# A hybrid decoder layer on one core: the input projection in column groups of 272, 512 and 256 instead of 272, 384 and 384, with padded activation rows

## The chip, the core and the metric

The kernel runs on one core of one Trainium2 chip. A core has a matrix engine (PE, TensorE), a vector engine (DVE, VectorE), a scalar engine (ACT, ScalarE), a general engine (POOL, GpSimd) and a queue that issues transfers (SP, SyncE). They share an on-chip memory of 128 partitions (SBUF); PE writes its results to a second one (PSUM), which is used in banks of 512 fp32 values for each partition. The metric is the device time of one execution in microseconds. Before the change it is 1302.69 us, the median of three runs from 1301.43 to 1303.88.

## The reference

One layer: 16 meta tokens are put in front of 1024 tokens, so there are L = 1040 rows. They are normalised and projected to seven groups of columns, which feed two mixers side by side; then come an output projection and a feed-forward network with a short convolution.

```python
h = jnp.concatenate([meta, x], axis=1)
a = rmsnorm(h, ln_mix_pre[l])
proj = a @ w_in[l]
dq, dk, dv, hq, hf, hi, hg = jnp.split(proj, SPLITS, axis=-1)
y_diff = diff_attention(dq, dk, dv, ...)
y_hgrn = hgrn2(hq, hf, hi, hg, ...)          # uses silu(hg) as a gate
mix = jnp.concatenate([y_diff, y_hgrn], axis=-1) @ w_out[l]
h = h + rmsnorm(mix, ln_mix_post[l])
a = rmsnorm(h, ln_ffn_pre[l])
y = conv_ffn(a, w_ffn_up[l], ffn_conv_w[l], ffn_conv_b[l], w_ffn_down[l])
h = h + rmsnorm(y, ln_ffn_post[l])
```

All data are fp32. There are 4 attention heads (dq, dk, dv) and 4 recurrent heads (hq, hf, hi, hg); each of the seven has 128 columns for a head.

## The kernel before

**Tiles.** The 1040 rows are 9 blocks, one of 16 and eight of 128. The normalised rows are kept transposed: `ahi` and `alo` hold, for each of 8 slices k of the 1024 features, 1040 columns; `ahi` is the value rounded to PE's fast fp32 form, `alo` what the rounding left. The weights are split in the same way into a high and a low part (`load_split`: ACT casts the high part, POOL subtracts). A product then takes three matmuls for each k: high by high (L241), high by low (L243), low by high (L245). One projected tile is 128 columns of the result by all 1040 rows, and is made in three column groups (`GROUPS`): blocks 0 to 2 (272 columns), 3 to 5 (384) and 6 to 8 (384). `proj_group` takes a PSUM bank of the tag `ip` for a group, issues its 24 matmuls through `proj_step`, and then calls the tile's own function (`evac`) that copies the result out. There are 28 such tiles, seven for each of the four heads.

**Stages.** Head 0's dq, dk and dv are made while the rows are still being normalised and transposed. This stage's beginning is written out by hand with the class `Kinds` (L893): group 0 of the three tiles and group 1 of dq, between the transposes (L280) of blocks 3, 4 and 5. Then `head0(1)` is interleaved with blocks 6 to 8 (`pre_blocks`), and `head0(2)` with the tables of the position bias. Then, for each head h, the tiles hf, hq, hi and hg are interleaved with the attention of head h, and dq, dk and dv of head h+1 with the recurrence of head h. In these stages there are two banks of the tag `ip`, so a group may start once the group before the last has been copied out. The output projection follows (L1020, L1022, L1024), in two halves of 512 columns (n = 0 and 1), with its weights loaded and split by `load_wo`; then the feed-forward network (L1383 to L1385 up, L1543 to L1545 down).

**Order.** PE's instructions run in the order in which the code issues them; `interleave` hands out dense matmuls against the small ones by a cost in ns. The other engines' order is chosen by a scheduler from a model of costs, except for the written-out beginning. So a change in widths or buffers can move instructions on ACT, DVE and POOL that the diff doesn't name.

**Names that the prediction uses.** xs is a block of rows: ACT squares and sums it (`pre_stat`), takes ln and exp of the sum ss, DVE scales it (`pre_scale`), PE transposes it into px (`pre_turn`), ACT and DVE copy px to `ahi` and `alo`. sg and gate belong to hg: `ev_g` runs exp on ACT, a bound on DVE, two more steps on ACT and the product with the PSUM bank on DVE. woh, wol and wor are the high part, the low part and the raw load of the output weights, wh_dk and wr_dk the same for dk's; ws and ra are sums and raw loads of the up weights. Raw loads of weights go round a ring of three buffers (tag `wr`). The split output weights n = 0, k = 2 to 4 and n = 1, k = 6 and 7 lie in a pool of their own (`wosplit`), opened ahead of `ahi` and `alo`; those of n = 0, k = 0 and 1 lie with the other weights, and the rest in a pool that is opened when `ahi` and `alo` are gone, and so have to wait for the last dense matmul.

## Time and profile before

| what | value |
|---|---|
| median of 3 runs | 1302.69 us |
| lowest, highest | 1301.43, 1303.88 us |
| time of the profiled execution | 1300.73 us |
| its span | 1298.9 us |
| PE busy | 1268.1 us, 98% |
| DVE, ACT, POOL busy | 887.0, 695.1, 482.6 us |

The span runs from the first to the last instruction that the profiler saw. A row of the timeline gives the start in us, the duration in us, the engine, the line, the operation, what is written from what, the shape and the number of like instructions; in brackets stands how long the engine was idle before, and what ended the idle time. L53 is the line of a helper through which all of ACT's, DVE's and POOL's instructions pass, so these are told apart by their tiles. Rows of the table by stage give, after the length, the busy time and the number of instructions of PE, of PE's weight loads, DVE, ACT and POOL, then the granted clock of PE as a share of full speed, the DMA engines' busy share and the GB/s. Rows of the waits give the waiting engine and line, what it waited for, the total in us, the number of waits and the longest. A row of one tile gives the number of instructions, the least, median and greatest duration in ns, the first and last start, and the shapes.

### The profile page before, as it was taken

How to read it: one execution, taken by the hardware profiler on the slowest of the kernel's cores; microseconds unless marked ns; L12 is line 12 of the kernel's file. 1: busy time of each engine (PE TensorE's matmuls, PEld its weight loads, DVE VectorE, ACT ScalarE, POOL GpSimd, SP SyncE). 2: the span in 40 equal slices, each digit the busy share in tenths (PEclk: the TensorE clock that was granted, in tenths of full speed). 3: DMA queues.
4: the chain of work that ended last, by engine and by line, in shares of the span. 5: the costliest groups of instructions: out<-in, count | busy, mean ns of one | idle time of the engine just before them, and what ended most of it. 6: DMA issues, size and time to landing. Idle time of an engine off the chain costs nothing.

```text
span 1298.9 us, 26100 instructions
## 1 busy us (share of the span) xinstructions
PE 1268.1 (98%) x10154; PEld 1179.0 (91%) x10154; DVE 887.0 (68%) x1488; ACT 695.1 (54%) x1639; POOL 482.6 (37%) x387
## 2 busy tenths in 40 slices
PE   8999999999999999999999999999999999999996
PEld 7999999899999998767899999999999998888885
DVE  7574646465645574547897877778778767697686
ACT  8465466546654764356854544544445435554553
POOL 5231423242323310353066575666665731010121
PEclk9999999999999999999999999999999999999999
DMA  6244655182644532787312222222222128964263
GB/s 215 94 99 89 120 120 116 47 156 78 125 116 86 122 103 90 222 272 265 117 67 82 90 75 82 74 89 83 74 75 90 66 79 274 336 203 170 90 211 122
DMA packets 116418, 165.04 MB, mean 127 GB/s; under 512 B 10099, under 2 KB 57523, under 8 KB 116294
## 3 DMA queue, kind: packets, MB, share of 16 engines
q1 hardware_dynamic: 93062, 151.84, 35.1%
q0 software_dynamic: 23232, 11.54, 7.6%
q8 instruction: 80, 1.31, 0.4%
q14 instruction: 44, 0.36, 0.1%
HBM read 134.24 MB, written 52.17 MB: 144 GB/s over the span
## 4 chain that ended last, share of the span: by engine, by line
PE 46%; DVE 4%; ACT 2%; issue 1%; DMA 1%; DVEq 0%; ACTq 0%
PE pd L1544 5%; PE pd L1545 5%; PE pd L1543 5%; PE pb L1383 5%; PE pb L1384 4%; PE pb L1385 4%; PE pa L1384 3%; PE pa L1383 3%; PE pa L1385 3%; PE pc L1384 3%; PE pc L1383 3%; PE pc L1385 3%; DVE c L53 1%; DVE t L53 1%; DVE xh L53 1%
## 5 line engine op out<-in xcount | busy, mean ns | idle before, releaser
L1383 PE MATMUL pb<-t,uh 128*128 128x258 f32 x504 | 142.5, 283 | 2.9 <-DVE u L53 2.7
L1384 PE MATMUL pb<-t,uh 128*128 128x258 f32 x504 | 141.2, 280 | 0.0
L1385 PE MATMUL pb<-t,ul 128*128 128x258 f32 x504 | 141.0, 280 | 0.0
L1544 PE MATMUL pd<-wl,gh 128*128 128x512 f32 x308 | 120.5, 391 | 2.0 <-DVE wl L53 2.0
L1545 PE MATMUL pd<-wh,gl 128*128 128x512 f32 x308 | 120.0, 390 | 0.0
L1543 PE MATMUL pd<-wh,gh 128*128 128x512 f32 x308 | 120.0, 390 | 0.0
L53 DVE SCALAR_TENSOR_TENSOR c<-uu,cwt,c 128x514 f32<-128x514 f32 (+1 forms) x88 | 96.5, 1096 | 19.6 <-ACT c L53 18.9
L53 POOL TENSOR_TENSOR c<-c,c 128x514 f32<-128x514 f32 (+1 forms) x44 | 63.8, 1449 | 122.3 <-ACT c L53 120.2
L1383 PEld LDWEIGHTS pb<-t,uh 128*128 128x128 f32 x504 | 95.0, 189 | 5.3 <-DVE u L53 5.3
L1385 PEld LDWEIGHTS pb<-t,ul 128*128 128x128 f32 x504 | 95.3, 189 | 0.0
L1384 PEld LDWEIGHTS pb<-t,uh 128*128 128x128 f32 x504 | 95.0, 188 | 0.0
L1384 PE MATMUL pa<-t,uh 128*128 128x258 f32 (+1 forms) x336 | 94.7, 282 | 0.0
L1383 PE MATMUL pa<-t,uh 128*128 128x258 f32 (+1 forms) x336 | 94.6, 281 | 0.0
L1385 PE MATMUL pa<-t,ul 128*128 128x258 f32 (+1 forms) x336 | 94.3, 281 | 0.0
L1384 PE MATMUL pc<-t,uh 128*128 128x258 f32 (+1 forms) x336 | 94.1, 280 | 0.0
L1385 PE MATMUL pc<-t,ul 128*128 128x258 f32 (+1 forms) x336 | 94.1, 280 | 0.0
L1383 PE MATMUL pc<-t,uh 128*128 128x258 f32 (+1 forms) x336 | 93.9, 279 | 0.0
L53 DVE SCALAR_TENSOR_TENSOR c<-ug,cwt,c 128x514 f32<-128x514 f32 (+1 forms) x88 | 88.3, 1004 | 1.4 <-ACT c L53 0.6
L53 ACT CAST uh<-ra 128x512 fp32r<-128x512 f32 x67 | 41.1, 617 | 63.2 <-PE pb L1384 42.0
L53 DVE TENSOR_TENSOR ul<-ra,uh 128x512 fp32r<-128x512 f32 x42 | 40.2, 957 | 48.7 <-ACT uh L53 48.7
L53 POOL TENSOR_TENSOR ul<-ws,uh 128x512 fp32r<-128x512 f32 x42 | 60.4, 1437 | 34.4 <-ACT uh L53 33.7
L1544 PEld LDWEIGHTS pd<-wl,gh 128*128 128x128 f32 x308 | 57.8, 188 | 15.5 <-DVE wl L53 3.7
(388 smaller groups left out, 4167.1 us busy)
## 6 DMA issues: line engine op xcount, KB each, us to landing
ra<-in_wup_dram SPq DMA_DIRECT2D x88, 256.0 KB, 2.6
mp<-msc SPq DMA_DIRECT2D x23, 512.0 KB, 5.0
tsc<-in_wdown_dram SPq DMA_DIRECT2D x44, 256.0 KB, 4.5
wi<-tsc SPq DMA_DIRECT2D x44, 256.0 KB, 2.7
gi<-gsc SPq DMA_DIRECT2D x33, 256.0 KB, 4.4
wi<-in_wdown_dram SPq DMA_DIRECT2D x33, 256.0 KB, 5.2
gsc<-c SPq DMA_DIRECT2D x22, 257.0 KB, 2.0
tsc<-in_wdown_dram POOLq DMA_DIRECT2D x22, 256.0 KB, 7.4
```

The lines of the kernel that those rows point to most:

```text
L53: ins = call(*args, **kw)
L1383: T.matmul(pt, hi[:, s], th[:, k], start=(first and k == 0), stop=False, skip_group_check=True)
L1384: T.matmul(pt, hi[:, s], tl[:, k], start=False, stop=False, skip_group_check=True)
L1385: T.matmul(pt, lo[:, s], th[:, k], start=False, stop=(k == 3), skip_group_check=True)
L1543: T.matmul(py, gh[:, s], wh, start=(k == 0 and pr not in (3, 7)), stop=False, skip_group_check=True)
L1544: T.matmul(py, gh[:, s], wl, start=False, stop=False, skip_group_check=True)
L1545: T.matmul(py, gl[:, s], wh, start=False, stop=(k == NH - 1), skip_group_check=True)
```

## The change

The 25 tiles outside head 0's dq, dk and dv are made in groups of 272, 512 and 256 columns (`SPANS`), those three in four groups of 272, 256, 256 and 256 (`FIRST`). `ahi` and `alo` get rows of 4608 bytes instead of 4160: `place` puts 64 columns of space ahead of block 3 and 48 more ahead of block 7, and a gap of 128 bytes goes ahead of the tiles. The tiles ht, sg, vt and kn become 512 wide. The ring of raw weights has four buffers (`WR`) instead of three. The pool `wosplit` is opened after `ahi` and `alo` are closed. `gpo` and the squares at the end move to other tags. Head 0's groups 1 and 2 are interleaved with blocks 6 to 8, group 3 with the tables.

```diff
--- before.py
+++ after.py
@@ -29,9 +29,12 @@
 BIG = 9.0e18
 NEG = -3.0e38
 GROUPS = [(0, 3), (3, 6), (6, 9)]
+SPANS = [(0, 3), (3, 7), (7, 9)]
+FIRST = [(0, 3), (3, 5), (5, 7), (7, 9)]
 WN = [258, 256]
 C0 = [0, 514]
 FA, FH, FO = 840, 800, 740
+WR = 4
 
 
 def start(i):
@@ -40,6 +43,10 @@
 
 def rows(i):
     return META if i == 0 else P
+
+
+def place(t):
+    return t + (0 if t < start(3) else 64 if t < start(7) else 112)
 
 
 class Ordered:
@@ -153,7 +160,7 @@
             lows.append(low)
 
     def load_split(src, name, where=None, bufs=4):
-        raw = wp.tile([P, 512], F32, tag="wr", name=f"wr_{name}", bufs=3)
+        raw = wp.tile([P, 512], F32, tag="wr", name=f"wr_{name}", bufs=WR)
         hi = (where or wp).tile([P, 512], F32R, tag="wh", name=f"wh_{name}", bufs=bufs)
         lo = (where or wp).tile([P, 512], F32R, tag="wl", name=f"wl_{name}", bufs=bufs)
         last_load.append(SY.dma_start(raw, src))
@@ -186,9 +193,9 @@
             SY.dma_start(msc[b0:b1, :, l, P * k:P * k + P].rearrange("b p c -> p b c"),
                          m[:, l, off:off + P * n].bitcast(F32).rearrange("p (b c) -> p b c", c=P))
 
-    ws_cm, wsp = pool("wosplit", 6)
     at_cm, atp = pool("at", 1)
-    ahi, alo = (atp.tile([P, KD, L], F32R, tag=t, name=t) for t in ("ahi", "alo"))
+    gap(atp, "edge", 128)
+    ahi, alo = (atp.tile([P, KD, place(L - 1) + 1], F32R, tag=t, name=t) for t in ("ahi", "alo"))
 
     last_load, lows = [], []
@@ -226,8 +233,8 @@
     def load_m(m, name, where=None, bufs=4):
         return [load_split(win[m][:, 512 * c: 512 * (c + 1)], f"{name}_{c}", where, bufs) for c in range(2)]
 
-    def proj_group(g, parts, name, evac):
-        b0, b1 = GROUPS[g]
+    def proj_group(g, parts, name, evac, spans=SPANS):
+        b0, b1 = spans[g]
         t0, t1 = start(b0), start(b1 - 1) + P
         n = t1 - t0
         pt = ps_in(f"pi_{name}_{g}")
@@ -238,11 +245,12 @@
         cost = max(115.0, 0.42 * (t1 - t0))
         hi, lo = parts[k // 4]
         s = slice(P * (k % 4), P * (k % 4 + 1))
-        T.matmul(pt, hi[:, s], ahi[:, k, t0:t1], start=(k == 0), stop=False)
+        ts = slice(place(t0), place(t0) + t1 - t0)
+        T.matmul(pt, hi[:, s], ahi[:, k, ts], start=(k == 0), stop=False)
         yield cost
-        T.matmul(pt, hi[:, s], alo[:, k, t0:t1], start=False, stop=False)
+        T.matmul(pt, hi[:, s], alo[:, k, ts], start=False, stop=False)
         yield cost
-        T.matmul(pt, lo[:, s], ahi[:, k, t0:t1], start=False, stop=(k == KD - 1))
+        T.matmul(pt, lo[:, s], ahi[:, k, ts], start=False, stop=(k == KD - 1))
         if k == KD - 1:
             evac()
         yield cost
@@ -279,7 +287,7 @@
             k = 4 * half + j
             T.transpose(pt[:, j * r:(j + 1) * r], xss[i][:r, P * k: P * (k + 1)], ident[:r, :r])
         pv = pt[:, : 4 * r].rearrange("p (k t) -> p k t", k=4)
-        return pv, slice(4 * half, 4 * half + 4), slice(start(i), start(i) + r)
+        return pv, slice(4 * half, 4 * half + 4), slice(place(start(i)), place(start(i)) + r)
 
     def pre_hi(pv, ks, s):
         return A.copy(ahi[:, ks, s], pv)
...
@@ -885,16 +893,17 @@
     class Kinds:
         def __init__(self, j, g, bank):
             self.j, self.g = j, g
-            self.t0, self.t1 = start(GROUPS[g][0]), start(GROUPS[g][1] - 1) + P
+            self.t0, self.t1 = start(FIRST[g][0]), start(FIRST[g][1] - 1) + P
+            self.a0 = place(self.t0)
             self.pt = bank(f"pi_{tiles[j][1]}_{g}")[:, : self.t1 - self.t0]
 
         def part(self, half, w, a, first=False, last=False):
             for k in range(4 * half, 4 * half + 4):
-                T.matmul(self.pt, parts[self.j][half][w][:, P * (k % 4): P * (k % 4 + 1)], a[:, k, self.t0:self.t1],
+                T.matmul(self.pt, parts[self.j][half][w][:, P * (k % 4): P * (k % 4 + 1)], a[:, k, self.a0:self.a0 + self.t1 - self.t0],
                          start=bool(first and k == 0), stop=bool(last and k == KD - 1))
 
         def out(self):
-            tiles[self.j][2](self.g, *GROUPS[self.g], self.t0, self.t1, self.pt)
+            tiles[self.j][2](self.g, *FIRST[self.g], self.t0, self.t1, self.pt)
 
     def block(i):
         outs = [pre_turn(i, half, ps_m(f"px{i}_{half}")) for half in range(2)]
@@ -947,20 +956,24 @@
         for j, (m, name, evac) in enumerate(tiles):
             if (j, g) == (0, 1):
                 continue
-            for step, c in enumerate(proj_group(g, parts[j], name, evac)):
+            for step, c in enumerate(proj_group(g, parts[j], name, evac, FIRST)):
                 if step == 8:
                     flush()
                 yield c
 
+    def heads(*gs):
+        for g in gs:
+            yield from head0(g)
+
     def pre_blocks(bs):
         for i in bs:
             yield from pre_block(i)
 
-    interleave(head0(1), [pre_blocks([6, 7, 8])], 2400, 0)
+    interleave(heads(1, 2), [pre_blocks([6, 7, 8])], 2400, 0)
     with tc.issue_after(last_lo.ins):
         smalls()
         lam_terms()
-    interleave(head0(2), [bias_tables()], 2600)
+    interleave(heads(3), [bias_tables()], 1800)
     close(z_cm, p_cm)
     p_cm, pp = pool("ps", 2, space=PSUM)
     deep.update(ip=2, m=2)
@@ -980,8 +993,9 @@
             interleave(dense(tiles_a, None, wd_sums), [hgrn_head(t_h)] + carried(), FH, 1500)
 
     close(at_cm)
+    ws_cm, wsp = pool("wosplit", 6)
+    gap(wsp, "gap0", 448)
     wo_cm, wop = pool("wo", 7)
-    gap(wop, "gap0", 448)
     ml_cm, mlp = pool("mixload", 1)
     y_cm, yp = pool("y0", 1)
     y0 = yp.tile([P, NBLK, 512], F32, tag="y0", name="y0")
...
@@ -1132,7 +1146,7 @@
                 SY.dma_start(raws[nm], wup[m][:, 512 * c: 512 * (c + 1)])
 
     def w_sum(nm, a, b, op):
-        sums[nm] = wp.tile([P, 512], F32, tag="wr", name=f"ws{nm}", bufs=3)
+        sums[nm] = wp.tile([P, 512], F32, tag="wr", name=f"ws{nm}", bufs=WR)
         G.tensor_tensor(sums[nm], a, b, op=op)
         return sums[nm]
@@ -1179,7 +1193,7 @@
     m7 = ep.tile([P, 8 * WN[0]], F32R, tag="e1", name="m7")[:, 16:].rearrange("p (b l t) -> p b l t", b=8, l=2)
     for i in range(1, NBLK):
         SY.dma_start(m7[:, i - 1].bitcast(F32), msc[i][:, :, P * (KD - 1):])
-    gpo = qp.tile([P, 512], F32, tag="gpo", name="gpo", bufs=1)
+    gpo = parts_tile("gpo").bitcast(F32).rearrange("p l c -> p (l c)")[:, :512]
     SY.dma_start(gpo, gpost[:, 512:].to_broadcast([P, 512]))
     gfb = qp.tile([P, D], F32, tag="gfb", name="gfb", bufs=1)
     SY.dma_start(gfb, gfpre.to_broadcast([P, D]))
@@ -1547,7 +1561,7 @@
     hhs = {}
 
     def squares(src, m, c):
-        sq = fp.tile([P, 512], F32, tag="sq", name=f"sq{m}_{c}")
+        sq = wp.tile([P, 512], F32, tag="wr", name=f"sq{m}_{c}", bufs=WR)
         A.activation(sq, src, AF.Square, accum_out=ssd[:, m, c:c + 1])
 
     def rstd(m, c):
```

The order changes with it. In what follows, a name ends in a number of its own.

ACT in head 0 before, from block 6's square (xs_429, ss_430) to the first copy of its transposes; xs_472 and xs_515 are blocks 7 and 8, q the copy of dq's group 1:

```order
L53 ACTIVATE xs_429,ss_430<-xt_173 128x1024
L53 COPY vt_0_407<-pi_dv_0_349 128x272
L53 ACTIVATE ss_430<-ss_430,eps 128x1
L53 ACTIVATE xs_472,ss_473<-xt_234 128x1024
L53 ACTIVATE ss_430<-ss_430 128x1
L53 ACTIVATE xs_515,ss_516<-xt_306 128x1024
L53 ACTIVATE q_0_122<-pi_dq_1_394 64x384
L53 ACTIVATE q_0_123<-pi_dq_1_394 64x384
L53 CAST ahi<-px_0_436 128x4x128
```

The same place now (block 6 is xs_427 and ss_428, block 7 xs_476, block 8 xs_525):

```order
L60 COPY vt_0_405<-pi_dv_0_347 128x272
L60 ACTIVATE xs_427,ss_428<-xt_171 128x1024
L60 ACTIVATE xs_476,ss_477<-xt_232 128x1024
L60 ACTIVATE q_0_120<-pi_dq_1_392 64x256
L60 ACTIVATE q_0_121<-pi_dq_1_392 64x256
L60 ACTIVATE ss_428<-ss_428,eps 128x1
L60 ACTIVATE ss_477<-ss_477,eps 128x1
L60 ACTIVATE ss_428<-ss_428 128x1
L60 ACTIVATE xs_525,ss_526<-xt_304 128x1024
L60 ACTIVATE ss_477<-ss_477 128x1
```

The two copies of dq moved ahead of the ln and exp of block 6's sum. On PE, in both, block 6's transposes follow dq's last matmul of this group directly.

ACT at the end of the first head's hg before, from the first step on the middle group's bank to that of the last group:

```order
L53 ACTIVATE sg_1_1528<-pi_hg_1_1475 128x384
L53 ACTIVATE sg_1_1528<-sg_1_1528,one 128x384
L53 ACTIVATE sg_1_1528<-sg_1_1528 128x384
L53 CAST wh_dk_0_1585<-wr_dk_0_1584 128x512
L53 CAST wh_dk_1_1591<-wr_dk_1_1590 128x512
L53 ACTIVATE sg_2_1559<-pi_hg_2_1534 128x384
```

The same place now:

```order
L60 ACTIVATE sg_1_1615<-pi_hg_1_1569 128x512
L60 ACTIVATE sg_1_1615<-sg_1_1615,one 128x512
L60 CAST wh_dk_0_1672<-wr_dk_0_1671 128x512
L60 ACTIVATE sg_1_1615<-sg_1_1615 128x512
L60 CAST wh_dk_1_1678<-wr_dk_1_1677 128x512
L60 ACTIVATE sg_2_1646<-pi_hg_2_1621 128x256
```

The cast of the first half of dk's weights moved from behind the middle group's last step to ahead of it. On PE, the 24 matmuls of hg's last group and then dq's first group follow one another without other work, before and now. The same holds for the two heads that follow.

POOL at the second half of the output weights before, where ul is the low part of an up weight:

```order
L53 TENSOR_TENSOR ul_7001<-ra_22_6982,uh_7000 128x512
L53 TENSOR_TENSOR wol_6_7043<-wor_6_7040,woh_6_7042 128x512
L53 TENSOR_TENSOR wol_4_7031<-wor_4_7028,woh_4_7030 128x512
L53 TENSOR_TENSOR ws_7813<-ra_21_7809,ra_22_7807 128x512
L53 TENSOR_TENSOR ul_7880<-ws_7813,uh_7879 128x512
L53 TENSOR_TENSOR ws_7847<-ws_7813,ra_11_7805 128x512
```

The same place now:

```order
L60 TENSOR_TENSOR ul_7091<-ra_22_7072,uh_7090 128x512
L60 TENSOR_TENSOR wol_6_7133<-wor_6_7130,woh_6_7132 128x512
L60 TENSOR_TENSOR ws_7903<-ra_21_7899,ra_22_7897 128x512
L60 TENSOR_TENSOR ws_7937<-ws_7903,ra_11_7895 128x512
L60 TENSOR_TENSOR ul_7970<-ws_7903,uh_7969 128x512
L60 TENSOR_TENSOR wol_4_7121<-wor_4_7118,woh_4_7120 128x512
```

The low part of slice 4 moved behind two sums and one low part of the up weights. On ACT, the cast of slice 7 moved up to right behind that of slice 6.

ACT at the end of the last dense tile now, where woh_2, 3 and 4 are casts that ran among the dense tiles of the last head before:

```order
L60 ACTIVATE sg_1_6309<-sg_1_6309,one 128x512
L60 ACTIVATE sg_1_6309<-sg_1_6309 128x512
L60 CAST woh_2_6383<-wor_2_6381 128x512
L60 ACTIVATE sg_2_6340<-pi_hg_2_6315 128x256
L60 CAST woh_3_6389<-wor_3_6387 128x512
L60 CAST woh_5_6401<-wor_5_6399 128x512
L60 ACTIVATE sg_2_6340<-sg_2_6340,one 128x256
L60 CAST woh_4_6395<-wor_4_6393 128x512
```

The first of the casts stands ahead of the last gate's first step, the others among its steps.

16 lines of the change are left out of this document (8 added, 8 removed).

## The prediction

> **What bounds the kernel now.** I read the page's busy line first, then the table by stage, then PE's waits, then the timeline at the places that the change touches.
>
> ```profile
> span 1298.9 us, 26100 instructions
> PE 1268.1 (98%) x10154; PEld 1179.0 (91%) x10154; DVE 887.0 (68%) x1488; ACT 695.1 (54%) x1639; POOL 482.6 (37%) x387
> 100.00:600.00 500.00, 491.68 (x4755) 455.67 (x4754) 283.11 (x594) 272.73 (x786) 149.87 (x138) 1.00 0.52 128
> PE pt L715 <- DVE at L53: 2.3, 4, 1.0
> PE pa L739 <- ACT pb L53: 1.9, 3, 0.8
> ```
>
> PE is busy for 1268.1 of 1298.9 us, at a granted clock of 1.00. In 100 to 600 us, where nearly all the regrouped projections run, it is idle for only 8.3 us. So the time can change in two ways only: the start-to-start distance of PE's matmuls, and idle time of PE that comes or goes. DVE, ACT and POOL matter where PE waits for them; the last two rows are the attention's waits, the longest of the kind in that stretch.
>
> **What one matmul costs.** The duration that a row gives includes the overlap with the next one, so I use the distance of starts in stretches without other work.
>
> ```profile
> 127.71 0.34 PE L241 MATMUL pi_hg<-ahi,wh_hg 128*128 128x384 f32 x1
> 131.94 0.29 PE L241 MATMUL pi_dq<-ahi,wh_dq 128*128 128x272 f32 x1
> 133.45 0.29 PE L241 MATMUL pi_dq<-ahi,wh_dq 128*128 128x272 f32 x1
> 799.82 0.28 PE L1383 MATMUL pa<-t,uh 128*128 128x256 f32 x1
> 801.19 0.28 PE L1383 MATMUL pb<-t,uh 128*128 128x258 f32 x1
> 802.62 0.28 PE L1383 MATMUL pb<-t,uh 128*128 128x256 f32 x1
> 804.04 0.28 PE L1383 MATMUL pc<-t,uh 128*128 128x258 f32 x1
> 1099.94 0.39 PE L1543 MATMUL pd<-wh,gh 128*128 128x512 f32 x1
> 1105.61 0.39 PE L1544 MATMUL pd<-wl,gh 128*128 128x512 f32 x1
> 562.12 0.39 PE L1020 MATMUL py<-woh,mp 128*128 128x512 f32 x1
> 568.33 0.39 PE L1020 MATMUL py<-woh,mp 128*128 128x512 f32 x1
> ```
>
> Between the first two rows lie 24 matmuls of 384 columns: 4.23 / 24 = 176 ns. Then 12 of 272: 1.51 / 12 = 126 ns. In the FFN 12 of 256 take 1.37 us at one place and 1.42 us at another, 114 and 118 ns each, and in the down projection 25 of 512 take 5.67 us, 227 ns each. In the output projection 27 of 512 take 6.21 us, 230 ns each.
>
> **The regrouping.** A tile needs 24 such sets (8 k, 3 terms), with 1040 columns in each. Before, a set costs 126 + 176 + 176 = 478 ns; with 272, 512 and 256 columns, 126 + 227 + 116 = 469 ns (116 is the middle of the FFN's two). That is 9 ns times 24 sets times 25 tiles = 5.4 us saved. No matmul and no column goes away: what is saved is the cost beside the columns, and it depends on the 512-wide ones running here as they do in the down projection, with padded rows and other addresses. Bounds: nothing saved, if what is beyond the columns stays (478 ns); 126 + 227 + 114 = 467, 6.6 us. Head 0's three tiles get four groups: 126 + 3 x 116 = 474 ns instead of 478, 72 sets, 0.3 us saved (bounds 0.1 lost at 118, 0.7 saved at 114). The split output weights move in SBUF; if half of those matmuls fall from 230 to 227 ns, some 100 x 3 ns = 0.3 us is saved (bounds 0 and 0.7).
>
> [...]
>
> **Block 6 of the input, head 0.** The narrow dq group of head 0 stands right ahead of block 6's transposes on PE.
>
> ```profile
> 27.56 1.57 PE L893 MATMUL pi_dq<-alo,wh_dq 128*128 128x384 f32 x8
> 28.97 1.55 PE L893 MATMUL pi_dq<-ahi,wl_dq 128*128 128x384 f32 x8
> 30.40 1.29 PE L280 MATMUL px<-ident,xs 128*128 128x128 f32 x8
> 34.82 1.23 PE L280 MATMUL px<-ident,xs 128*128 128x128 f32 x8 [0.18 <-DVE xs L53]
> 26.56 1.06 ACT L53 ACTIVATE xs<-xt 128x1024 f32<-128x1024 f32 x1
> 28.04 0.30 ACT L53 ACTIVATE ss<-ss,eps 128x1 f32<-128x1 f32 x1
> 28.24 1.05 ACT L53 ACTIVATE xs<-xt 128x1024 f32<-128x1024 f32 x1
> 29.28 0.19 ACT L53 ACTIVATE ss<-ss 128x1 f32<-128x1 f32 x1
> 30.56 0.98 ACT L53 ACTIVATE q<-pi_dq 64x384 fp32r<-64x384 f32 x2
> 29.50 1.42 DVE L53 SCALAR_TENSOR_TENSOR xs<-xt,ss,gb 128x512 f32<-128x512 f32 x2 [0.84 <-ACT ss L53]
> ```
>
> Now ACT ends block 6's statistics (28.04, 29.28) before the copy of dq (30.56), DVE scales it at 29.50, and the transposes begin at 30.40 without a wait. In the changed order the copy of dq comes first, so the statistics' last steps wait for dq's end. With 256 columns dq's 24 matmuls take 24 x 114 = 2.7 us instead of 4.2, so dq ends 1.5 us earlier, at 28.9. ACT has the value copy and two Square passes first: v's end moves from 27.56 to about 27.1, then 0.4 + 1.0 + 1.1 us bring it to 29.7. The two copies of 256 columns take 0.75 (0.98 at 384), two small steps 0.45, the last 0.2: 31.1. DVE's first half takes 0.7: the transposes start at 31.9, and PE has waited since 28.9. That is 3.0 us lost. Bounds: 1.5 (start at 30.4 as now) and 3.5. Block 7's wait of 0.18 goes, since its statistics are now ready earlier.
>
> **The bank behind the gate.** Each head's last dense tile hg is followed by the next head's dq, whose first group takes the PSUM bank of hg's middle group.
>
> ```profile
> 127.91 0.49 ACT L53 ACTIVATE sg<-pi_hg 128x384 f32<-128x384 f32 x1 [1.08 <-PE pi_hg L245]
> 129.91 0.61 ACT L53 CAST wh_dk<-wr_dk 128x512 fp32r<-128x512 f32 x1
> 130.04 0.56 DVE L53 TENSOR_TENSOR gate<-pi_hg,sg 128x384 f32<-128x384 f32 x1 [1.24 <-ACT sg L53]
> L53 ACT ACTIVATE sg<-pi_hg x12: 397/484/492, 120.7 to 507.8; 128x384 f32<-128x384 f32 x8, 128x272 f32<-128x272 f32 x4
> L53 DVE TENSOR_SCALAR sg<-sg x12: 301/360/1154, 121.1 to 508.3; 128x384 f32<-128x384 f32 x8, 128x272 f32<-128x272 f32 x4
> L53 ACT ACTIVATE sg<-sg,one x12: 522/616/619, 121.4 to 508.7; 128x384 f32<-128x384 f32 x8, 128x272 f32<-128x272 f32 x4
> L53 ACT ACTIVATE sg<-sg x12: 430/524/527, 122.0 to 509.8; 128x384 f32<-128x384 f32 x8, 128x272 f32<-128x272 f32 x4
> L53 DVE TENSOR_TENSOR gate<-pi_hg,sg x12: 441/557/558, 122.5 to 510.5; 128x384 f32<-128x384 f32 x8, 128x272 f32<-128x272 f32 x4
> ```
>
> The bank is free when the gate's product has read it: 130.04 + 0.56 = 130.60, 2.9 us after the middle group ended (127.71). The last group covers 4.2 us (131.94), so nothing waits now. After the change the last group has 256 columns and covers 24 x 114 = 2.7 us, and the chain is longer: from 272 to 384 columns its five steps grow by 87 + 59 + 94 + 94 + 116 = 450 ns, so for 128 more, 0.5 us. The cast of wh_dk, which now stands behind the chain, moves in between its last two ACT steps: 0.55 us more. 2.9 + 0.5 + 0.55 - 2.7 = 1.2 us of waiting, at three turnovers (after the fourth head no dq follows): 3.6 us lost. Bounds 0.6 each (the cast costs nothing, 256 columns at 118), 1.8, and 1.3 each, 3.9.
>
> **The second half of the output weights.**
>
> ```profile
> 564.17 1.28 POOL L53 TENSOR_TENSOR wol<-wor,woh 128x512 fp32r<-128x512 f32 x1 [15.67 <-ACT woh L53]
> 566.48 1.29 POOL L53 TENSOR_TENSOR wol<-wor,woh 128x512 fp32r<-128x512 f32 x1 [1.02 <-ACT woh L53]
> 567.85 1.61 POOL L53 TENSOR_TENSOR ws<-ra,ra 128x512 f32<-128x512 f32 x1
> 569.24 0.39 PE L1022 MATMUL py<-wol,mp 128*128 128x512 f32 x1
> 572.25 0.40 PE L1020 MATMUL py<-woh,m 128*2 128x512 f32 x1 [0.55 <-ACT woh L53]
> 573.31 0.39 PE L1022 MATMUL py<-wol,m 128*2 128x512 f32 x1 [0.66 <-DVE wol L53]
> ```
>
> POOL makes the low parts of slices 6 (564.17) and 4 (566.48) and then FFN sums; PE takes slice 4 at 569.24. In the changed order two sums and one low part, 1.6 + 1.3 + 1.3 us, stand between: slice 4 is ready at about 565.4 + 4.2 + 1.3 = 570.9, 1.7 us late. On the other hand slice 7, for which PE waits 0.55 and 0.66 now, is cast right after slice 6, and with four raw buffers its load needn't wait for slice 4's: 1.2 us saved. Net 0.5 lost, bounds 1.2 saved and 3 lost.
>
> **The rest.** In the attention the middle groups' copies on ACT are some 0.1 us longer, three or so to a head ahead of a step of the softmax or norm that PE waits for: 1.0 us over four heads; bounds 1.5 saved (some of the waits shown above go) and 2.5 lost. Slices 2 to 4 of the first output weights are split only once the activations are dead: PE has 12 matmuls on slices 0 and 1 first, 12 x 230 = 2.8 us, against 0.6 + 0.7 us for the first cast and low part and as much for each next, so 0. The fourth raw buffer moves one FFN sum of a round earlier on POOL, which has slack there (37% busy): 0, bounds 1 either way.
>
> **Sum**, against the profiled span of 1298.9: -5.4 - 0.3 - 0.3 + 3.0 - 0.2 + 3.6 + 0.5 + 1.0 = +1.9 us. The profiled execution took 1300.73; the median of the runs is 1302.69 (1301.43 to 1303.88). So 1304.6 for the median.
>
> **The rivals.**
> - *The regrouping pays and the waits stay small.* Saved 6.6 + 0.7 + 0.7 at best, and the 1.2 of slice 7; lost 1.5 at block 6 and 1.8 at the turnovers: -5.9, some 1296.8. For it: the steady 227 ns of the down projection. Against it: the order of ACT, which nothing softens.
> - *512 columns cost their share here.* [...] For it: 230 rather than 227 ns in the output projection, so that a 512-wide matmul doesn't always run at its best. It decides from 236 ns on, where 126 + 236 + 116 is 478.
> - *The late split of the first output weights stalls PE.* If the last gate's steps (2.9 us) go ahead of the three casts and low parts, slice 2 is ready at 2.9 + 1.3 = 4.2 us instead of 2.8: 1.4 us more, and as much again if slice 4 suffers: +4.7, 1307.4. Against it: the order puts the first cast ahead of the gate's.
> - *The change doesn't do what it says.* Not seen: the widths stand in PE's order.
>
> **How the numbers follow.** Forecast 0.40, the first rival 0.24, the second 0.25, the third 0.11. A measurement tells no change up to about 0.2% (2.6 us, 1300.1 to 1305.3). The forecast's own range is 1302 to 1307: 0.24 within, 0.16 above. The first rival gives 0.23 faster and 0.01 within, the second 0.24 slower, 0.01 within, the third 0.08 slower, 0.03 within. Faster 0.23, the same 0.29, slower 0.48. The range reaches to the middles of the two outer cases, and leaves out about half of each: 1296.5 to 1310.5.
>
> **What would show it.** 512-column groups at 227 ns and 256 at 114 to 118 between starts; a PE wait of about 3 us for DVE's xs near 29 to 32; waits of about 1.2 us of pi_dq for DVE's gate at three turnovers; the wait for slice 7 gone, one for POOL's slice 4 in its place. PE's matmul distance of 236 ns or more at 512 columns, or no such waits, would make the prediction wrong.

## The result and the profile after

| | before | after |
|---|---|---|
| median of 5 runs each | 1302.69 us | 1316.28 us |
| lowest, highest | 1300.95, 1303.88 | 1313.75, 1319.52 |
| span of the profiled execution | 1298.9 us | 1311.9 us |

The change made the kernel slower: the ratio is 1.0107, with a 95% interval from 1.0095 to 1.0120. That is 13.6 us between the medians and 13.0 us between the two profiled spans.

The head of the page of the changed kernel, and its busy line:

```profile
span 1311.9 us, 26213 instructions
PE 1266.8 (97%) x10226; PEld 1155.6 (88%) x10226; DVE 895.6 (68%) x1492; ACT 690.2 (53%) x1647; POOL 478.3 (36%) x387
```

PE's busy time hardly moved (1268.1 before), so nearly all of the loss is idle time of PE. The table by stage tells where. Its three rows run from the first projection matmul to the first of head 0's hf, from there to head 1's dq, and from there to the output projection. First before, then after:

```profile
11.70:57.76 46.06, 44.31 (x277) 40.54 (x276) 31.93 (x64) 31.14 (x72) 20.51 (x22) 1.00 0.42 143
57.76:131.94 74.18, 73.10 (x502) 70.99 (x502) 40.57 (x97) 44.68 (x135) 18.88 (x17) 1.00 0.39 86
131.94:507.61 375.67, 370.79 (x3706) 356.58 (x3706) 216.15 (x481) 212.43 (x617) 108.17 (x104) 1.00 0.48 104
```

```profile
11.80:62.30 50.50, 46.07 (x348) 43.73 (x348) 29.64 (x64) 32.48 (x79) 18.93 (x18) 0.97 0.38 128
62.30:141.06 78.76, 73.34 (x503) 66.73 (x501) 42.08 (x102) 44.96 (x136) 20.95 (x21) 1.00 0.44 100
141.06:517.14 376.08, 367.24 (x3706) 333.77 (x3706) 222.51 (x478) 206.61 (x613) 106.15 (x105) 1.00 0.47 99
```

The first number behind the stretch is its length, the second PE's busy time. The first stage grew by 4.4 us: 2.7 more of idle time, and 1.8 more of busy time with a granted clock of 0.97 in place of 1.00. The second grew by 4.6, of which 4.3 is idle time. In the third, PE is 3.6 us less busy, which is the saving that was meant, and 4.0 us more idle. So 9.5 of the 13.0 us are lost before the output projection starts. That stage itself adds 0.8, the up projection of the feed-forward network (FFN) 2.1, the down projection and what follows 0.6.

PE's waits in the changed kernel name what it waited for:

```profile
PE pb L1397 <- DVE u L60: 4.7, 9, 1.7
PE px L288 <- DVE xs L60: 4.1, 2, 3.2
PE ssa L589 <- ACT ona L60: 3.7, 4, 1.0
PE pt L723 <- ACT pb L60: 2.6, 4, 0.7
PE pi_dq L249 <- DVE gate L60: 2.5, 3, 0.9
PE pa L1251 <- DVE a L60: 2.4, 3, 1.0
PE py L1036 <- POOL wol L60: 2.2, 1, 2.2
PE pl L475 <- DVE hq L60: 2.1, 3, 0.7
PE S L666 <- DVE rb L60: 2.0, 1, 2.0
```

Here rb is a table of the position bias, ona the attention's output on its way to its norm, u an intermediate result that DVE makes in the FFN, a the rows that PE transposes ahead of the FFN, and pl a product of the recurrence. The waits for xs (block 6), for the gate and for slice 4's low part `wol` were predicted; those for `rb` and `ona`, the many for `u`, and those of pl for hq were not. (L60 is now the helper's line that was L53.)

**Block 6, and a clock that fell behind it.** The timeline around block 6's statistics in the changed kernel:

```profile
29.70 0.75 ACT L60 ACTIVATE q<-pi_dq 64x256 fp32r<-64x256 f32 x2
30.86 0.19 ACT L60 ACTIVATE ss<-ss 128x1 f32<-128x1 f32 x1
31.37 2.74 DVE L60 SCALAR_TENSOR_TENSOR xs<-xt,ss,gb 128x512 f32<-128x512 f32 x4
32.27 1.29 PE L288 MATMUL px<-ident,xs 128*128 128x128 f32 x8 [3.20 <-DVE xs L60]
34.16 0.42 PE L253 MATMUL pi_dk<-ahi,wl_dk 128*128 128x256 f32 x1
34.37 0.41 PE L249 MATMUL pi_dk<-ahi,wh_dk 128*128 128x256 f32 x1
```

The copy of dq (29.70), the statistics' last step (30.86), the scaling (31.37) and the transposes (32.27) follow each other as the prediction had them. But the last two rows start 0.21 us apart, where 256 columns take 0.118 us among the gate's rows below. The windows of two microseconds show why; PE's granted clock is the third number from the end:

```profile
30.00:32.00 2.00, 0.00 (x0) 0.00 (x0) 1.48 (x3) 1.96 (x8) 0.00 (x0) 1.00 0.00 0
32.00:34.00 2.00, 1.70 (x13) 1.52 (x14) 2.00 (x4) 1.95 (x8) 0.00 (x0) 0.94 0.00 0
34.00:36.00 2.00, 2.00 (x11) 2.00 (x11) 1.97 (x4) 0.39 (x3) 0.00 (x0) 0.50 0.01 4
36.00:38.00 2.00, 2.00 (x15) 2.00 (x14) 1.47 (x9) 0.41 (x2) 0.00 (x0) 0.71 0.00 0
```

By the trace's record of the clock it falls to one half at 33.76 us, soon after the pause, and returns at 37.17. The windows sum to 2 x (0.06 + 0.50 + 0.29) = 1.7 us of full speed lost, all of it in "busy" time. The stall at block 6 therefore cost 3.2 + 1.7 us.

**The bias tables.** The tables of the position bias, on PE before and after (the first of the four), and what waits for the last of them:

```profile
42.63 0.44 PE L346 MATMUL pb<-oh,tbb 64*128 64x384 f32 x1
```

```profile
51.50 0.44 PE L354 MATMUL pb<-oh,tbb 64*128 64x384 f32 x1
67.53 0.56 DVE L60 COPY rb<-pb 128x384 f32<-128x384 f32 x1 [4.60 <-DMA rsc<-rb]
68.15 0.34 PE L666 MATMUL S<-k,q 128*128 128x144 f32 x1 [2.03 <-DVE rb L60]
```

The change spreads the tables over the last group of head 0's three tiles, which now has 256 columns instead of 384, so the first begins 8.9 us later. The DVE copy of each of the other three waits for the transfer of the table before it, 7.4 us in all (4.60 for the last): the last copy stands at 67.53, and head 0's first scores wait 2.03 us for it.

**The gate's bank.** The chain at the first turnover in the changed kernel:

```profile
137.22 0.28 PE L249 MATMUL pi_hg<-ahi,wh_hg 128*128 128x256 f32 x1
137.42 0.60 ACT L60 ACTIVATE sg<-pi_hg 128x512 f32<-128x512 f32 x1 [3.53 <-PE pi_hg L253]
139.14 0.60 ACT L60 CAST wh_dk<-wr_dk 128x512 fp32r<-128x512 f32 x1
139.65 0.63 ACT L60 ACTIVATE sg<-sg 128x512 f32<-128x512 f32 x1
139.93 0.28 PE L253 MATMUL pi_hg<-ahi,wl_hg 128*128 128x256 f32 x1
140.31 0.69 DVE L60 TENSOR_TENSOR gate<-pi_hg,sg 128x512 f32<-128x512 f32 x1 [1.83 <-ACT sg L60]
141.06 0.40 PE L249 MATMUL pi_dq<-ahi,wh_dq 128*128 128x272 f32 x1 [0.85 <-DVE gate L60]
```

The cast of wh_dk stands inside the chain, as predicted, and PE waits for the bank; 0.85 us and not 1.2. The first and the fifth row are 23 matmuls apart: 2.71 / 23 = 118 ns for 256 columns, the upper end of what was taken.

**The norm of the attention.** ACT ahead of PE's transpose of the attention's output (`ssa`), in head 1:

```profile
209.84 0.41 ACT L60 ACTIVATE f<-kr 128x256 f32<-128x256 f32 x1
210.41 0.58 ACT L60 ACTIVATE kr<-f,omlb,nomlb 128x256 f32<-128x256 f32 x1
210.90 0.24 ACT L60 COPY ona<-pa 128x128 f32<-128x128 f32 x1
211.19 0.23 PE L589 MATMUL ssa<-ident,ona 16*128 16x16 f32 x1 [0.96 <-ACT ona L60]
```

f and kr are the copy-out of hf, which takes five steps on ACT. The narrow group's now follows right behind the wide one's on ACT, and the copy to ona stands among them. PE loses some 0.9 us here in each head; before, ssa is not among PE's waits.

**Slice 4 of the output weights.**

```profile
573.67 1.29 POOL L60 TENSOR_TENSOR wol<-wor,woh 128x512 fp32r<-128x512 f32 x1 [15.91 <-PE py L1036]
575.03 1.62 POOL L60 TENSOR_TENSOR ws<-ra,ra 128x512 f32<-128x512 f32 x1
579.22 1.71 POOL L60 TENSOR_TENSOR wol<-wor,woh 128x512 fp32r<-128x512 f32 x1
580.98 0.50 PE L1036 MATMUL py<-wol,mp 128*128 128x512 f32 x1 [2.16 <-POOL wol L60]
```

POOL makes the FFN's sums `ws` between the two low parts, and PE waits 2.16 us for the second. The waits for slice 7 (0.55 and 0.66 before) are gone.

### The profile page after: what moved, and what is told of

Its sections match the earlier page's. It is cut to its first block, busy times and chain, and to the rows that moved or that the text cites. A ratio compares the mean times of both kernels' runs of the same rounds, so it can differ in the third digit from the quotient of the medians.

```text
span 1311.9 us, 26213 instructions
## 1 busy us (share of the span) xinstructions
PE 1266.8 (97%) x10226; PEld 1155.6 (88%) x10226; DVE 895.6 (68%) x1492; ACT 690.2 (53%) x1647; POOL 478.3 (36%) x387
## 4 chain that ended last, share of the span: by engine, by line
PE 37%; DVE 11%; ACT 3%; issue 3%; DMA 1%; DVEq 0%; ACTq 0%
PE pd L1558 5%; PE pd L1559 5%; PE pd L1557 4%; DVE c L60 4%; PE pb L1397 4%; PE pb L1398 3%; PE pb L1399 3%; PE pa L1398 2%; PE pa L1397 2%; PE pa L1399 2%; PE pc L1398 2%; PE pc L1397 2%; PE pc L1399 2%; DVE ul L60 2%; DVE t L60 1%
## 5 line engine op out<-in xcount | busy, mean ns | idle before, releaser
L60 DVE SCALAR_TENSOR_TENSOR c<-uu,cwt,c 128x514 f32<-128x514 f32 (+1 forms) x88 | 96.5, 1096 | 19.7 <-ACT c L60 19.0
L60 POOL TENSOR_TENSOR c<-c,c 128x514 f32<-128x514 f32 (+1 forms) x44 | 63.9, 1451 | 120.9 <-ACT c L60 118.9
L60 DVE SCALAR_TENSOR_TENSOR c<-ug,cwt,c 128x514 f32<-128x514 f32 (+1 forms) x88 | 88.5, 1007 | 1.4 <-ACT c L60 0.6
L60 ACT CAST uh<-ra 128x512 fp32r<-128x512 f32 x67 | 41.1, 616 | 66.7 <-PE pb L1398 42.5
L60 DVE TENSOR_TENSOR ul<-ra,uh 128x512 fp32r<-128x512 f32 x42 | 41.7, 994 | 49.4 <-ACT uh L60 49.4
L60 POOL TENSOR_TENSOR ul<-ws,uh 128x512 fp32r<-128x512 f32 x42 | 58.6, 1396 | 39.4 <-ACT uh L60 21.7
```

Of the source, the lines that this page charges most:

```text
L60: ins = call(*args, **kw)
```

## The experiments

The diffs are against the changed kernel. Kernels in one comparison share a chip and runs of the kernel before; ratios are to that kernel, with 95% intervals.

**e1: all groups as before, the rest of the change kept.**

```diff
-SPANS = [(0, 3), (3, 7), (7, 9)]
-FIRST = [(0, 3), (3, 5), (5, 7), (7, 9)]
+SPANS = GROUPS
+FIRST = GROUPS
-    return t + (0 if t < start(3) else 64 if t < start(7) else 112)
+    return t + (0 if t < start(3) else 64 if t < start(6) else 112)
-    interleave(heads(1, 2), [pre_blocks([6, 7, 8])], 2400, 0)
+    interleave(heads(1), [pre_blocks([6, 7, 8])], 2400, 0)
-    interleave(heads(3), [bias_tables()], 1800)
+    interleave(heads(2), [bias_tables()], 2600)
```

> Changed kernel with every column group as before (272, 384, 384, head 0 too, its interleaving too); padded rows, four raw buffers, 512-wide tiles and the moved pool of split output weights stay. Theory A (the loss is made of waits that the new widths bring in head 0's stage and among the dense tiles, some 11 of the 13 us): before plus 2 us, about 1305. Rival B (buffers, pool and padding cost the time in the later stages and by their addresses): 1310 or more.

Measured: 1309.25 us, ratio 1.0058 (1.0043 to 1.0073). The output projection starts 1.4 us earlier than in the kernel before, so nothing is lost up to there; the loss is all behind it. The regrouping is not the only cause: something in "the rest", which the prediction had at next to nothing, costs half a per cent.

**e2: only head 0's four groups; the other tiles as before.**

```diff
-SPANS = [(0, 3), (3, 7), (7, 9)]
+SPANS = GROUPS
-    return t + (0 if t < start(3) else 64 if t < start(7) else 112)
+    return t + (0 if t < start(3) else 64)
```

> Changed kernel with the 25 dense tiles in groups of 272, 384 and 384 as before; head 0's three tiles keep their four groups and their interleaving; padding of 64 columns ahead of block 3 alone. Theory A: head 0's part is 3.2 us at block 6, 2.0 us at the bias tables and 1.6 us of matmul distance, with 2 us of the rest: about 1311, of which PE's wait for block 6 (about 3 us) and for the bias tables (about 2 us) are seen. Rival B: 1315. Rival C (nearly all is in the 25 dense tiles): 1305.

Measured: 1312.57 us, 1.0094 (1.0076 to 1.0113). Head 0's part alone takes head 0's hf to +4.6 us, as in the changed kernel (+4.5): the block 6 stall and its clock.

**e3: only the regrouping of the other 25 tiles; head 0 as before.**

```diff
-FIRST = [(0, 3), (3, 5), (5, 7), (7, 9)]
+FIRST = GROUPS
-    return t + (0 if t < start(3) else 64 if t < start(7) else 112)
+    return t + (0 if t < start(3) else 64)
-    interleave(heads(1, 2), [pre_blocks([6, 7, 8])], 2400, 0)
+    interleave(heads(1), [pre_blocks([6, 7, 8])], 2400, 0)
-    interleave(heads(3), [bias_tables()], 1800)
+    interleave(heads(2), [bias_tables()], 2600)
```

> Changed kernel with head 0's three tiles in groups of 272, 384 and 384 and its interleaving as before; the 25 dense tiles keep 272, 512 and 256; padding of 64 columns ahead of block 3 alone. Theory A: waits for the gate 2.5 us, for the attention's norm 3.7 us and for the recurrence 2.5 us come, some 2 us of the old attention waits go, 2 us of matmul distance are saved, 2 us of the rest: about 1309. No wait for the bias tables, none of 3 us at block 6. Rival C: 1313 or more. Rival B: 1315.

Measured: 1310.15 us, 1.0067 (1.0050 to 1.0084). No loss at the start (hf at +0.1), 2.0 us in the second stage, 0.4 in the third, and then the rest's loss as in e1. Here, without the second gap in the rows, 272, 512 and 256 columns take 126, 232 and 118 ns: 476 ns a set, as before. Head 0's groups thus cost 0.36% more than the rest alone (e2 against e1), the regrouping of the 25 tiles 0.09% (e3 against e1), each uncertain by some 0.2; with the rest's 0.58% that is 1.03%, close to the change's 1.07.

**e4: no gaps in the rows.**

```diff
-    return t + (0 if t < start(3) else 64 if t < start(7) else 112)
+    return t
```

> Changed kernel with unpadded rows of 4160 bytes, all else as it is. Theory A: the waits stay and the 512-column matmuls lie a few ns further apart (230 ns now, 232 to 236 then; 256 at 118 to 120): 1316 to 1320. Rival D (the padding itself brings the loss, by other addresses): below 1310.

Measured: 1317.57 us, 1.0123 (1.0108 to 1.0139). Within one hg tile, 19 matmuls of 512 columns lie between these two rows, 4.40 / 19 = 232 ns:

```profile
133.07 0.39 PE L253 MATMUL pi_hg<-ahi,wl_hg 128*128 128x512 f32 x1
137.47 0.28 PE L249 MATMUL pi_hg<-ahi,wh_hg 128*128 128x256 f32 x1
```

And the window of its third stage:

```profile
141.34:517.41 376.07, 369.41 (x3706) 335.13 (x3707) 219.19 (x478) 206.87 (x613) 107.80 (x105) 1.00 0.46 100
```

By the medians of the distances inside a tile, a set costs 126 + 232 + 118 = 476 ns here and some 470 ns with the gaps (124 for 272 columns, 228 to 231 for 512 and 117 for 256, by which matmuls are counted). So by the distances the cut into 512 and 256 columns saves nothing by itself; the gaps save some 6 ns a set, 3.6 us for 600 sets. By PE's busy time the gaps save 2.2 us in the 21 tiles of the third stage (369.41 against 367.24), 2.6 us for all 25, and the cut alone 1.4 us there (369.41 against 370.79 before). And yet that stage is just as long with them (376.08) as without (376.07): pl's waits for DVE's hq, 2.1 us there in the changed kernel, are not in this kernel's table of that stretch. What the gaps saved, another wait gave back. The profiled execution of this run has half clock in three places, at block 6, behind slice 4's wait and behind a wait of 1.74 us for u, so its whole span is not compared.

**e5: e1 with a ring of three raw buffers.**

```diff
-WR = 4
+WR = 3
```

> As the run with only the rest of the change, and the ring of raw weights back to three buffers; padding, moved pool, wider tiles and moved tags stay. Theory A2 (the rest's 7.6 us are made by the fourth buffer alone, which lets the scheduler put the sums of up weights earlier on POOL, and so makes DVE late in every FFN round and slice 4 of the output weights late): before minus 0 to 1 us, no wait of PE for DVE's u but the first two, none for POOL's low part. Rival E (the late split, the moved tags or the padding make it): still 6 us or more above before.

Measured: 1302.69 us beside 1301.98, 1.0009 (0.9998 to 1.0019). With the ring as before, "the rest" costs nothing that can be told, so the fourth buffer cost e1 half a per cent (1.0058 to 1.0009, 6.4 us). PE's wait for u in e1, and the window of its up projection:

```profile
PE pb L1397 <- DVE u L60: 6.5, 15, 1.7
```

```profile
661.70:1084.64 422.94, 416.42 (x3506) 413.13 (x3505) 323.58 (x463) 199.43 (x359) 256.37 (x181) 1.00 0.24 82
```

The same two in e5:

```profile
PE pb L1397 <- DVE u L60: 2.7, 2, 1.4
```

```profile
659.78:1077.19 417.41, 414.45 (x3506) 412.28 (x3505) 321.23 (x463) 201.55 (x359) 261.07 (x182) 1.00 0.25 83
```

With a fourth buffer a raw load or a sum `ws` can come one step sooner, and the scheduler places the sums earlier on POOL: slice 4's low part falls behind them, and in the FFN the u of many rounds comes too late (15 waits instead of 2). That the fourth buffer does this is shown by the one-line edit; how POOL's order delays u was not followed step by step. Slice 4's wait, 2.2 us in e1, is not in e5's table either.

**e6: the changed kernel with a ring of three** (the same one-line edit).

> The changed kernel with three raw buffers instead of four and nothing else. Theory A2: 6 to 8 us less than the changed kernel, about 1308 where before is 1301 to 1303. Rival E: the same as the changed kernel within 2 us.

Measured: 1312.99 us, 1.0087 (1.0068 to 1.0106), 0.2% less than the changed kernel, though the intervals overlap. The third stage's and the start's losses stay (output projection at +10.1 us). In its profile the half clock at block 6 lasts, by the windows, from about 31.4 to 38.2 us, twice as long as in the changed kernel, which makes the start 1.1 us longer (head 0's hf at +5.6 us).

**e7: the narrow group in the middle, 272, 256 and 512 columns.**

```diff
-SPANS = [(0, 3), (3, 7), (7, 9)]
+SPANS = [(0, 3), (3, 5), (5, 9)]
-    return t + (0 if t < start(3) else 64 if t < start(7) else 112)
+    return t + (0 if t < start(3) else 64 if t < start(5) else 112)
```

> The changed kernel with the dense tiles in groups of 272, 256 and 512 instead of 272, 512 and 256, the padding moved with them. Theory A (the wait for the gate comes of a wide middle group ahead of a narrow last one): the three waits of PE for DVE's gate, 0.85 us each, are gone, and some of those for the attention's norm; 3 us less than the changed kernel. Rival F (a wait only moves to the next group): the same within 1 us, with waits elsewhere.

Measured: 1319.96 us, 1.0136 (1.0116 to 1.0156). This is slower. The groups start at other addresses, and 512 columns take 233 to 234 ns, 256 take 120: some 6 to 8 ns a set, about 4 us in all (PE's busy time in the third stage is 371.22 us instead of 367.24). The waits did get shorter (for the gate 1.4 us instead of 2.5), but by less than was expected. Its profile also shows a stretch of half clock behind slice 4's wait (see e14), which the changed kernel's first profile has not.

**e8: block 6's statistics and scaling ahead of dq's copy, and the tables spread over two groups.**

```diff
+        if i > 6:
...
+    stat[6] = pre_stat(6)
+    for half in range(2):
+        pre_scale(6, half, stat[6])
-    interleave(heads(1, 2), [pre_blocks([6, 7, 8])], 2400, 0)
+    interleave(heads(1), [pre_blocks([6, 7, 8])], 2400, 0)
-    interleave(heads(3), [bias_tables()], 1800)
+    interleave(heads(2, 3), [bias_tables()], 1800)
```

> The changed kernel with block 6's statistics and scaling written ahead of dq's copy in the ordered beginning, and with the bias tables interleaved with the last two groups of head 0 instead of the last. Theory A (both waits of head 0's stage come of the order): PE's wait for block 6 falls from 3.2 to about 2 us (block 7's square still stands ahead), the 2.0 us for the tables go: 3 us less than the changed kernel. Rival G (the waits are paid by the transfers of the tables and of x anyway): the same within 1 us.

Measured: 1313.88 us, 1.0096 (1.0079 to 1.0113). The window at block 6:

```profile
32.00:36.00 4.00, 3.96 (x35) 3.80 (x34) 3.89 (x8) 2.92 (x11) 0.00 (x0) 1.00 0.00 0
```

The pause is 2.1 us instead of 3.2 and the clock stays full; the wait for `rb` is gone as well. Head 1's dq stands at +3.7 us instead of +9.1. Then 3.2 us are lost in the output projection, where the changed kernel lost 0.8, and 3.7 in the FFN's up projection instead of 2.1. So the two causes at the start are confirmed by their stages, though the time of the whole shows little of it. Part of the loss in the output projection is a stretch of half clock behind slice 4's wait (see e14); the rest, and that of the up projection, wasn't followed further.

**e9: dk's second group issued ahead of block 6's transposes**, so that PE has work there.

```diff
-    interleave(heads(1, 2), [pre_blocks([6, 7, 8])], 2400, 0)
+    interleave(heads(1, 2), [pre_blocks([6, 7, 8])], 2400, 2800)
```

> The changed kernel with dk's second group of head 0 issued on PE ahead of block 6's transposes (2.8 us of dense work first) and nothing else. Theory A (PE only stands there because dq, now narrow, ends before block 6's statistics): the wait of 3.2 us for block 6 is gone and the time is 3 us less than the changed kernel's, about 1313. Rival G (the time is lost later in head 0's stage, since blocks 7 and 8 and the tables come later too): the wait for the bias tables grows from 2.0 us, and the time falls by 1 us or less.

Measured: 1310.23 us, 1.0065 (1.0049 to 1.0082). One number that gives PE 2.8 us of matmuls brings back 0.42%, 5.5 us: hf of head 0 starts at -0.2 us instead of +4.5, and the clock stays full there. In the repetition e16 it starts at 0.0.

**e10: e9, with the tables over two groups and a ring of three.**

```diff
-WR = 4
+WR = 3
-    interleave(heads(1, 2), [pre_blocks([6, 7, 8])], 2400, 0)
+    interleave(heads(1), [pre_blocks([6, 7, 8])], 2400, 2800)
-    interleave(heads(3), [bias_tables()], 1800)
+    interleave(heads(2, 3), [bias_tables()], 1800)
```

> The last kernel with the bias tables interleaved with the last two groups of head 0 and with three raw buffers. Theory A with A2 (block 6, the tables and the fourth buffer are separate losses): 3 + 2.4 + 3.3 = 8.7 us less than the changed kernel, about 1307; what is left above before, some 5 us, are the waits among the dense tiles and head 0's 72 additional matmuls. Rival H (they cover one another): 1310 or more.

Measured: 1304.56 us, 1.0031 (1.0021 to 1.0040). Three mended causes, block 6, the tables and the ring, take away 0.76 of the 1.07%.

**e11: e3 with a ring of three.**

> As the run with head 0 as before and the dense tiles in 272, 512 and 256 (padding ahead of block 3 alone), with three raw buffers instead of four. Theory A2 (the fourth buffer costs about 7 us behind the dense tiles): before plus 2 to 4 us, all of it made before the output projection. Rival E: before plus 7 or more, as with four buffers.

Measured: 1305.87 us, 1.0038 (1.0025 to 1.0051), 0.29% less than e3: the ring's price again.

**e12: e10, with hg in four groups.** Only hg, whose copy-out holds the bank longest, gets the widths of head 0:

```diff
-            for g in range(3):
-                for step, c in enumerate(proj_group(g, parts, name, evac)):
+            sp = FIRST if name[:2] in ("hg",) else SPANS
+            for g in range(len(sp)):
+                for step, c in enumerate(proj_group(g, parts, name, evac, sp)):
```

> The last fixed kernel (dk ahead of block 6, tables with two groups, three raw buffers), and the tile hg of each head in four groups of 272, 256, 256 and 256 instead of 272, 512 and 256 (24 more matmuls a tile, the same columns). Theory A (the wait for the gate comes of its 512-wide group): the three waits of 0.85 us are gone, those for the attention's norm stay: 2.5 us less than the last fixed kernel, about before plus 1.5 us. Rival F (the wait moves on): the same within 1 us.

Measured: 1301.72 us (median of 11 runs) beside 1301.08, 1.0007 (0.9997 to 1.0016). The waits of pi_dq for the gate (2.5 us in e10) are gone from the table of waits, and the kernel is as fast as the one before: 0.24% less than e10, 3.1 us, and 2.3 us between their spans.

**e13: e12, with hf in four groups too**, against the waits for ona.

> The same with hf in four groups too. Theory A (the norm waits on ACT behind the forget gate's steps on 512 and then 256 columns, all of a piece): the waits of PE for the attention's norm, 0.7 to 1.0 us in each of four heads, go as well: 2 to 3 us less again, before minus 1 to plus 0 us. Rival F: they come back at the attention's other steps, and the time is that of the kernel with hg alone within 1 us.

Measured: 1302.27 us, 1.0007 (0.9998 to 1.0016). The waits for ona left the list, but others took their place (pl for PE's own issue 2.4 us, pn_vh for DVE's ast 1.6), and the time is that of e12. Neither version beats the kernel before.

**e14, e15 and e16: the changed kernel, e3 and e9 once more, unaltered**, one execution of each beside one of the kernel before (1300.96). The clock had also fallen to one half elsewhere: in e9 from 576.5 us, right behind slice 4's wait of 2.17 us, and in e3 from 679.9 us, behind a wait of 1.77 us for u.

> The changed kernel once more, unaltered, on whichever chip comes, to see whether the stretches of half clock belong to the program or to the moment. Its first profile shows one: 0.50 from about 33.9 to 37.1 us, behind PE's wait of 3.2 us ahead of block 6; behind its wait of 2.16 us for slice 4's low part (580.98) the clock stayed at 1.00. [...] Theory B (the program decides): a drop at 33.9 us and no other, the span within 1 us of 1311.9.

> The kernel of e3 once more, unaltered. Its first profile shows a drop from about 679.9 to 683.3 us, behind a wait of 1.77 us for DVE's u, and none behind the wait of 2.17 us for slice 4 at 574.82. [...] Theory B: again at 680 us alone, the span within 1 us of 1308.9.

> The kernel of e9 once more, unaltered. Its first profile shows a drop from about 576.2 to 579.6 us, behind the wait of 2.17 us for slice 4, and none at the FFN's first waits. [...] Theory B: again at 576 us alone, the span within 1 us of 1308.9.

Measured: 1316.36, 1310.44 and 1315.49 us. In e14 the clock falls at block 6 again, and once more at 630 us, behind a wait of 3.6 us for the transfer of mp, an operand of the output projection; in e15 it falls at slice 4 and not at 680 us; in e16 not at slice 4 but at 628 us, behind a wait of 4.5 us for mp. (The waits for mp were 0.6 and 0.4 us in the first profiles of these two; the 4.1 us more of it are most of the 4.8 us between the spans of e16 and e9.) Slice 4 in e9 and then in e16:

```profile
576.25 0.63 PE L1036 MATMUL py<-wol,mp 128*128 128x512 f32 x1 [2.17 <-POOL wol L60]
```

```profile
578.25 0.51 PE L1036 MATMUL py<-wol,mp 128*128 128x512 f32 x1 [2.16 <-POOL wol L60]
```

The same program has the same wait, and from the second matmul behind it on the distance is 0.43 us in one execution and 0.24 in the other. So it is not the program alone that decides whether a slow stretch follows a pause of two microseconds. What differs between the two executions was not shown. The last section counts the pauses and the falls behind them over all traces.

## Why the prediction was wrong

The forecast was +1.9 us, the range up to 1310.5; measured were +13.6, 1316.28. The steps that failed are a cost that was put at nothing on an argument alone (the fourth buffer), two that the sum lacked (the bias tables and the half clock behind block 6), waits of the recurrence that it has no term for either, and a saving taken from the wrong cause. By the prediction's own steps:

- **Regrouping, -5.4: wrong in its reason.** It took the saving from what a matmul costs beside its columns. By the distances the cut alone saves nothing (476 ns before, in e3 and in e4), so the second rival, by which the regrouping saves nothing, was right on the cut. By PE's busy time it saves at most 1.4 us in the third stage. What is saved, 2.6 to 3.6 us, comes from the gaps in the rows, which the prediction named as an uncertainty and not as the source. That a set came out at some 470 ns, where 469 was forecast, is luck: the forecast took the 227 ns from the down projection, without the gaps in mind, and without them it was 232.
- **Block 6, +3.0: right in place and mechanism (3.2), and too small in effect.** The step counted idle time alone. The half clock behind it cost 1.7 more, so the term was 4.9; e9, which fills the pause, brought back 5.5.
- **Block 7's wait, -0.2, and head 0's groups, -0.3:** block 7's wait is gone, as predicted. The four groups saved nothing: 256 columns take 118 ns there, and PE's busy time in that stage, 46.07 less the clock's 1.7, is that of before (44.31).
- **The moved output weights, -0.3: as forecast.** In the output projection the median distance of 512 columns fell from 231 to 227 ns, and PE's busy time there by 0.4 us.
- **The gate's bank, +3.6: right in mechanism, too large in size.** Three waits of 0.85, 2.5 us; e12 takes them away and gains 2.3 to 3.1 us.
- **The tables: a term that was missing.** The prediction looked at the order of head 0's groups and not at what was spread over them: +2.0 us at the first scores. e8 and e10 removed it.
- **The fourth raw buffer, 0 with bounds of 1: a cost that was put at nothing.** It was argued that POOL has slack (37% busy). It has, but the order within it decided: 6.4 us with the old groups (e1 to e5), 3.7 in e3 to e11, and some 2.6 in the changed kernel, where the intervals overlap. Slice 4's lateness belongs to it.
- **The second half of the output weights, +0.5:** slice 4 late by 2.16 (1.7 was predicted), slice 7's waits gone as predicted. The half clock behind slice 4's wait comes on top in some executions: of the eleven that have this wait in their profile, it fell in six.
- **The attention, +1.0: near, and the recurrence missing.** PE's waits for its and the recurrence's small steps (ssa, pt, pl, pn_vh and, before, pa) sum to 9.7 us after and 5.8 before, +3.9. Of these the attention's steps are 7.2 after and 5.8 before, +1.4; the other 2.5 us are waits of pl in the recurrence, of which the prediction has no term. The reason given for the attention, copies that are 0.1 us longer, was not the one found: at ssa (3.7 us) copy-outs come close behind each other on ACT, and in e13, with hf in four groups, those waits are gone. e13 also shows that narrower groups here only move the wait. What delays hq for pl was not followed.
- **Late split of slices 2 to 4: 0,** as predicted: PE has no wait there.

By measured sizes: some -3 to -4 (gaps and cut), +4.9 (block 6), +2.0 (tables), +2.5 (gate), +3.9 (attention and recurrence), some +2.6 (ring, with slice 4) is +12 to +13, beside 13.0 between the spans. Terms overlap where one wait hides in another, so the sum is a check and no proof. The edits are stronger evidence: mending block 6, the tables and the ring takes away 0.76% (e10), mending the gate's bank another 0.24% (e12), and what is left of the 1.07% cannot be told from nothing.

Left open: why the waits of pa for a in front of the FFN grew from 0.9 to 2.4 us (in e14, the same kernel, they are 0.7, so they do not belong to the program alone); why the gaps act as they do, of which only the times were measured; and what the fourth buffer would cost the kernel before, which wasn't tried.

## What to carry to other kernels

Where PE is the bound and a pause of two or three microseconds is about to appear, look for other matmuls to issue into it (here one number, 2.8 us of a later group, was worth 5.5 us), and price the pause with the slow clock that may follow (1.7 us here). Before widening a group, compare the time that its copy-out holds the bank with the time of the next group; the tile with the longest copy-out can keep narrower groups. A bigger ring of buffers is a change of order: check where each engine's queue then puts what the bound engine waits for, whatever the engine's busy share.

## What the hardware showed unexpectedly

**The clock after a pause.** In the changed kernel PE's granted clock stood at 0.50 from 33.76 to 37.17 us, which cost 1.7 us of busy time. In the other profiles, up to the last matmul, each fall took 1.7 us of full speed as well by windows of 4 us, and the one in e6 at block 6 twice that (3.4). Behind the 3.2 us at block 6 the clock fell in all six profiles that have the pause, the changed kernel's two among them; behind slice 4's 2.2 us in six of eleven; behind the longest wait for u, 1.7 to 1.8 us, in two of those eleven (1.77 us in e3, 1.74 in e4); behind the waits for mp of 3.6 us (e14) and 4.5 us (e16); and not behind the 2.1 us at block 6 in e8, nor behind 2.3 us for mp in e3. So of a pause of some two microseconds these traces do not say beforehand whether a slow stretch will follow.

**The place of the moving rows.** By the medians, the same 512 columns took 228 to 231 ns with the change's gaps, 232 to 233 without gaps and 233 to 234 with the offsets of e7; 256 took 117, 118 and 120. Between the first two only the address in SBUF of the rows differs; e7 has another order of the groups as well. With 384 columns the gaps changed nothing (175 ns in e5).
